# A transformer block with experts on one core: all TensorE instructions held to the order of the program

## The chip, the cores and the metric

The kernel runs on one core of a Trainium2 chip. The core has five engines, each with its own queue of instructions: TensorE (PE, matmuls and transposes; PEld is its load of weights), VectorE (DVE), ScalarE (ACT), GpSimd (POOL) and SyncE (SP), which issues most of the transfers. The engines wait for each other by semaphores. The metric is the device time of one execution in microseconds (us), the median over several executions.

## The reference

The reference takes 512 tokens of 1024 features in fp32 through two hybrid layers and a third block:

```python
for l in range(2):
    x = x + 0.5 * swiglu_ffn(rms_norm(x, ffn1_norm_w[l]), ffn1_w_gate[l], ffn1_w_up[l], ffn1_w_down[l])
    x = x + hybrid_mixer(rms_norm(x, mix_norm_w[l]), l, w_in[l], w_out[l], ...)
    x = x + 0.5 * swiglu_ffn(rms_norm(x, ffn2_norm_w[l]), ffn2_w_gate[l], ffn2_w_up[l], ffn2_w_down[l])
```

`hybrid_mixer` projects the input, runs three branches beside each other (an mLSTM in chunks of 64, a state space model in chunks of 128, and differential attention with normalised q and k) and projects them back. The third block holds a token mixer, which is a gated delta rule in two directions (in each chunk of 64 a triangular system is solved, then states are carried from chunk to chunk) beside a pooling over a grid with windows of 2, 4, 8 and 16, a second delta rule over a context of 256 tokens that gives the states to begin with, and 16 experts, each of which takes the tokens that chose it most (twice 512 tokens over 16 experts, so 64 each).

## The kernel before

Every fp32 factor is held as two rounded parts, hi and lo, and each product takes three matmuls: hi by hi (L69), lo by hi (L70), hi by lo (L71), all in `mm3`. A projection (`fm_proj`) is 8 steps over the features by three, 24 matmuls of 128x512. `tok_proj` (L238 to L240) is the same with the operands exchanged. ACT casts each chunk of weights to hi (L39), DVE takes the difference lo (L40).

`scaled_x` (L138) prepares a normalised layer: ACT casts the scaled x (L146), DVE makes lo (L147), ACT squares x (L151), POOL adds the squares up (L155). `token_stats` sums them over the partitions on PE (L106, first one sum, then the other), DVE forms the inverse root (`rsqrt`, L81 to L88), `token_rows` brings it back to rows on PE (L120), and ACT copies it to `rb` (L128). The projections don't need `rb`, only their evictions do.

In `mixer` the first four projections are q and k. After each, DVE scales it (L321), ACT squares it (L323) and PE sums the squares by head (L325). `rows()` transposes small statistics (L355). The branches are generators which `Side.pump` advances by a step, placed by hand into the stream of projections: attention (L772 QK, L782 and before it the softmax, L758 the transposes two units later, L744 the product with v), the state space model, the mLSTM. At the end `turn()` transposes the results and the output projections follow.

In ffn2 of the second layer the side work is `context`: gates (L1195 transposes, then a chain of DVE instructions, L902, L903 and L914 on PE) and the solves. A solve runs on DVE row by row, writes its blocks to memory (L1069), reads them back in another layout (L1080), and multiplies them on PE in 64x64 matmuls (L1089, L1107, L1117); `delta_scan` carries the states (L1134). `token_mixer` does the same for the 512 tokens, with the pooling (L1341, L1358, L1378, L1379) beside it. `mixer_out` transposes the scan's output (L1430), which POOL leaves at L1426. `moe` gathers tokens (L1605), multiplies them with chunks of 1 MB (L1643), for which there are 17 places, and combines the results (L1661).

What sets the order: the program is traced by Python, and a scheduler then orders each engine's instructions. It takes the instruction traced first when several are ready by its own estimate of times, and lets one that is traced later pass one that it believes to be waiting. So the order of PE before is the scheduler's. Each queue runs in its order: a waiting matmul holds what is behind it.

Of the kernel before, what the change touches and what calls it, by code (L numbers as in the profile page):

```python
# [28 lines left out]
class G:  # L29
    pass  # L30

# [68 lines left out]
def token_stats(g, sqs, nt, pool):  # L100
# [3 lines left out]
    for j, sq in enumerate(sqs):  # L104
        for i in range(nt):
            nc.tensor.matmul(ps[:, 2 * i:2 * i + 2], sq[:, i * 128:(i + 1) * 128], g.ones[:, 0:2],  # L106
                             start=(i + j == 0), stop=False, skip_group_check=True)
# [7 lines left out]
def token_rows(g, rt):  # L115
# [3 lines left out]
    for i in range(nt):  # L119
        g.nc.tensor.matmul(pb[:, i * 128:(i + 1) * 128], bc(rt[:, i:i + 1], [128, 128]), g.ident, start=True, stop=True)  # L120
# [104 lines left out]
def tok_proj(g, xh, xl, w, cols, pump=lambda: None):  # L225
# [5 lines left out]
    for wh, wl in w:  # L231
        n = wh.shape[1]
        for i in range(NT):
            ts = slice(i * 128, (i + 1) * 128)
            o = ps[i][:, :cols]
            for k in range(n):
                kk = k0 + k
                nc.tensor.matmul(o, xh[:, kk, ts], wh[:, k, :], start=(kk == 0), stop=False)  # L238
                nc.tensor.matmul(o, xh[:, kk, ts], wl[:, k, :], start=False, stop=False)  # L239
                nc.tensor.matmul(o, xl[:, kk, ts], wh[:, k, :], start=False, stop=(kk == NK - 1))  # L240
# [49 lines left out]
def mixer(g, L, w_in, w_out):  # L290
# [25 lines left out]
    for e in range(2):  # L316
        w = chunk(256)
        for m in range(2):
# [5 lines left out]
            for i in range(NT):  # L324
                nc.tensor.matmul(pst[:, 16 * i + 4 * t:16 * i + 4 * t + 4], sq[:, i * 128:(i + 1) * 128], g.blk,  # L325
# [20 lines left out]
    def rows(v, name):  # L346
# [7 lines left out]
        for i in range(NT):  # L354
            nc.tensor.transpose(pt[0:2 * n, i * 128:(i + 1) * 128], f32(parts[:, i]).rearrange("p a b -> p (a b)"),  # L355
# [4 lines left out]
    def scale_qk():  # L360
        drT = rows(drn, "dr")
        yield
        for t in (2, 3, 0, 1):
            p = sm(g)
            nc.tensor.matmul(p, g.sel16[:, t, :], drT, start=True, stop=True)
# [16 lines left out]
    def gates():  # L382
# [10 lines left out]
        for i, m in enumerate((g.triu, g.ones)):  # L393
            nc.tensor.matmul(pc[:, 48 * i:48 * i + 48], m, dl.rearrange("p c h -> p (c h)"), start=True, stop=True)
# [92 lines left out]
    def turn(k):  # L487
        p = sm(g)
        for i in range(NT):
            nc.tensor.transpose(p[:, i * 128:(i + 1) * 128], ys[k // 2][:, i, (k % 2) * 128:(k % 2 + 1) * 128], g.ident)  # L490
# [27 lines left out]
def ssd(g, V, fm, G, ys):  # L518
# [7 lines left out]
    def product(todo):  # L526
# [4 lines left out]
        for hh in range(8):  # L531
            nc.tensor.matmul(py[:, hh * 64:(hh + 1) * 64], es[hh // 4][:, hh % 4, :], xc[:, hh, :],
                             start=True, stop=True)
        nc.vector.tensor_add(y, y, py)
        if c0:
            po = sm(g)
            for q in range(2):
                nc.tensor.matmul(po[:, q * 256:(q + 1) * 256], fm[6 + q][:, c0 * 128:(c0 + 1) * 128],
# [4 lines left out]
        if c0 < NT - 1:  # L543
            pst = sm(g)
            for q in range(2):
                nc.tensor.matmul(pst[:, q * 256:(q + 1) * 256], bt[:, q, :], xcd[:, 4 * q:4 * q + 4, :],
# [9 lines left out]
    for c in range(NT):  # L556
# [3 lines left out]
        for t in range(4):  # L560
            nc.tensor.transpose(px[:, t * 128:(t + 1) * 128], fm[t][:, ts], g.ident)
# [4 lines left out]
        if c < NT - 1:  # L566
            pb = sm(g)
            for q in range(2):
                nc.tensor.transpose(pb[:, q * 128:(q + 1) * 128], fm[4 + q][:, ts], g.ident)
# [7 lines left out]
        for q in range(2):  # L577
            nc.tensor.matmul(pcb[:, q * 128:(q + 1) * 128], fm[4 + q][:, ts], fm[6 + q][:, ts], start=True, stop=True)
# [3 lines left out]
        for q in range(2):  # L582
            pa = sm(g)
            e = g.scr()[:, :S].rearrange("p (h d) -> p h d", h=4)
            nc.tensor.matmul(pa.rearrange("p (h d) -> p h d", h=4), g.eye_r, bc(g.neg_r[:, None, :], [128, 4, 128]),
                             start=True, stop=False, skip_group_check=True)
            for h in range(4):
                hh = 4 * q + h
                nc.tensor.matmul(pa[:, h * 128:(h + 1) * 128], bc(g.stk8[:, hh:hh + 1], [128, 128]), acT[:, ts],
# [35 lines left out]
def mlstm(g, gt, G, qk, vx, ycat):  # L625
# [5 lines left out]
    for i in range(NT):  # L631
        nc.tensor.transpose(pt[0:4, i * 128:(i + 1) * 128], a[:, i, :], g.ident)
# [6 lines left out]
    for i in range(NT):  # L639
        nc.tensor.transpose(pg[:, 4 * i:4 * i + 4], Gr[:, i * 128:(i + 1) * 128], g.ident[0:4, 0:4])  # L640
# [7 lines left out]
    def product(h, P):  # L648
        pn = sm(g)
        for i in range(NT):  # L650
            for j in range(i + 1):
                nc.tensor.matmul(pn[:, 66 * i:66 * i + 66], P[j][:, (i - j) * 128:(i - j + 1) * 128], vx[:, j, h, :],
# [11 lines left out]
    for e in range(2):  # L664

        pGs = []
        for h in (2 * e, 2 * e + 1):
            pG = sm(g)
            nc.tensor.matmul(pG, bc(g.stk4[:, h:h + 1], [128, 128]), Gs, start=True, stop=True)
# [4 lines left out]
        for j in range(NT):  # L674
# [3 lines left out]
            for r in range(2):  # L678
                pr = slice(64 * r, 64 * r + 64)
                pq = sm(g)  # L680
                nc.tensor.matmul(pq[:, :W], qk[1, e][pr, js], qk[0, e][pr, j * 128:], start=True, stop=True)
# [37 lines left out]
def attention(g, V, ks, qkd, dv, ycat):  # L719
# [17 lines left out]
    for n in range(len(units) + 3):  # L737
        if n >= 3:
# [4 lines left out]
            for j in range(i + 1):  # L743
                nc.tensor.matmul(po[:, h * 64:(h + 1) * 64], aT[:, j * 128:(j + 1) * 128], dv[:, j, h, :],  # L744
# [7 lines left out]
        if 2 <= n < len(units) + 2:  # L752
# [4 lines left out]
            for j in range(i + 1):  # L757
                nc.tensor.transpose(pT[:, j * 128:(j + 1) * 128], pr[:, j * 128:(j + 1) * 128], g.ident)  # L758
# [3 lines left out]
        if n < len(units):  # L762
# [7 lines left out]
            for e in range(2):  # L770
                p = sm(g)
                nc.tensor.matmul(p[:, :W], qt[0:96, h // 2, 2 * (h % 2) + e], ks[2 * h + e][0:96, 0:W],  # L772
# [25 lines left out]
def modulation(g, I):  # L798
# [14 lines left out]
    for b in range(3):  # L813
# [11 lines left out]
        for i, acc in enumerate(accs):  # L825
# [6 lines left out]
            for j in range(4):  # L832
                nc.tensor.matmul(p[32 * j:32 * j + 32, 0:16], fold, r[:, j:64:4], start=True, stop=True)
# [39 lines left out]
def delta_gates(g, ab, nt, pool, pre):  # L873
# [26 lines left out]
    for i, src in enumerate((a, rest)):  # L900
        for d, tri in ((0, g.triu), (1, g.tril)):
            nc.tensor.matmul(pv[:, 0, i, :, 4 * d:4 * d + 4], tri, src[:, :, 4 * d:4 * d + 4], start=True, stop=True)  # L902
        nc.tensor.matmul(pv[:, 1, i], g.ones, src, start=True, stop=True)  # L903
# [9 lines left out]
    for i in range(nt):  # L913
        nc.tensor.transpose(pt[0:32, i * 128:(i + 1) * 128], f32(parts[:, i]).rearrange("p a b -> p (a b)"), g.ident)  # L914
# [31 lines left out]
def prep_keys(g, kraw, nt, P, kt, kf):  # L946
# [4 lines left out]
    for h in range(4):  # L951
        sq = P["scr"]()[:, :nt * 128]
        nc.scalar.activation(sq, kraw[h], AF.Square)
        for c in range(nt):
            nc.tensor.matmul(pq[:, 4 * c + h:4 * c + h + 1], sq[:, c * 128:(c + 1) * 128], g.ones[:, 0:1],
# [1093 lines left out]
```

## Time and profile before

| | us |
|---|---|
| median of 3 executions | 3054.05 (3049.53 to 3057.12) |
| profiled execution | 3055.56 |
| its span | 3053.5 |
| mean granted TensorE clock | 0.969 |

The span is the time from the first to the last instruction of the profiled execution; 2.06 us lie outside it. The granted clock is a share of the full 2.4 GHz. Stretches by start: ffn1 of the first layer to 396 us, its mixer to 686, ffn2 from 690, the second layer's ffn1 from 1059, its mixer from 1427, ffn2 with the context from 1724, the token mixer from 2166, its output and the routing from 2460, the experts from 2572 us.

### The profile page before, as it was taken

The page shows a single profiled execution, that of the slowest core. Times are in us where ns is not written, and L with a number is a line of the kernel's source. Part 1 is how long each engine was busy: PE and PEld are TensorE (multiplying, and loading weights), DVE is VectorE, ACT ScalarE, POOL GpSimd, SP SyncE. Part 2 cuts the span into 40 slices and gives each one's busy share as a digit, 9 for nine tenths or more (in the row PEclk, how much of TensorE's full clock was granted, in tenths as well). Part 3 has the DMA queues.
Part 4 walks back from the last instruction along what each step waited for, and adds up shares of the span by engine and source line. Part 5 has one row for each costly group of instructions (what it writes and reads, how often), then busy time and mean ns, then how long its engine had stood idle before and what let it go on. Part 6 is the DMA issues. An engine that isn't in the chain of part 4 may idle for free. (4 is left out here: it accounts for less than half of the span.)

```text
span 3053.5 us, 37758 instructions
## 1 busy us (share of the span) xinstructions
PE 2905.0 (95%) x15232; PEld 2225.9 (73%) x15232; DVE 1636.6 (54%) x2847; ACT 905.5 (30%) x1515; POOL 321.4 (11%) x260
## 2 busy tenths in 40 slices
PE   7999998999999999999999999999998877999998
PEld 6888887877888888888776788888787765444444
DVE  4445457665444598545676666454765643122213
ACT  3222334543222332223354433222342321010002
POOL 0001012110201102011210201201100110000000
PEclk9999999999999999999998999999999978999998
DMA  4432343122332358224421233222323435999996
GB/s 146 126 100 92 104 147 116 52 85 84 97 97 94 113 197 297 99 93 135 128 76 56 93 114 104 84 85 90 114 66 94 116 142 201 394 419 418 418 418 277
DMA packets 293107, 472.03 MB, mean 155 GB/s; under 512 B 45215, under 2 KB 237471, under 8 KB 269508
## 3 DMA queue, kind: packets, MB, share of 16 engines
q1 hardware_dynamic: 290216, 466.28, 43.4%
q10 hardware_dynamic: 2716, 3.34, 0.3%
q8 instruction: 120, 1.97, 0.3%
q14 instruction: 55, 0.45, 0.0%
HBM read 449.90 MB, written 19.67 MB: 154 GB/s over the span
## 5 line engine op out<-in xcount | busy, mean ns | idle before, releaser
L69 PE MATMUL mm<-xh,whi 128*128 128x512 f32 x1952 | 777.0, 400 | 12.0 <-ACT xh L146 8.4
L70 PE MATMUL mm<-xl,whi 128*128 128x512 f32 x1952 | 774.9, 397 | 0.6 <-DVE xl L147 0.6
L71 PE MATMUL mm<-xh,wlo 128*128 128x512 f32 x1952 | 772.5, 396 | 1.7 <-DVE wlo L40 1.7
L39 ACT CAST whi<-wraw 128x1024 fp32r<-128x1024 f32 (+3 forms) x390 | 390.9, 1003 | 1113.8 <-PE mm L70 831.4
L40 DVE TENSOR_TENSOR wlo<-wraw,whi 128x1024 fp32r<-128x1024 f32 (+3 forms) x390 | 501.6, 1286 | 97.5 <-ACT whi L39 90.5
L69 PEld LDWEIGHTS mm<-xh,whi 128*128 128x128 f32 x1952 | 372.5, 191 | 92.2 <-ACT xh L146 9.3
L70 PEld LDWEIGHTS mm<-xl,whi 128*128 128x128 f32 x1952 | 372.9, 191 | 82.0 <-issue 3.8
L71 PEld LDWEIGHTS mm<-xh,wlo 128*128 128x128 f32 x1952 | 372.4, 191 | 80.6 <-DVE wlo L40 3.3
L69 PE MATMUL mm<-hh,whi 128*128 128x512 f32 x704 | 279.4, 397 | 0.0
L70 PE MATMUL mm<-hl,whi 128*128 128x512 f32 x704 | 278.7, 396 | 0.0
L71 PE MATMUL mm<-hh,wlo 128*128 128x512 f32 x704 | 278.4, 395 | 0.0
L192 POOL TENSOR_TENSOR x<-x,dt 128x512 f32<-128x512 f32 x72 | 125.7, 1746 | 859.7 <-DVE dt L191 766.0
L172 DVE TENSOR_TENSOR gs<-mm,rb 128x512 f32<-128x512 f32 x88 | 60.8, 691 | 202.5 <-PE mm L71 198.2
L191 DVE SCALAR_TENSOR_TENSOR dt<-mm,rb 128x512 f32<-128x512 f32 x104 | 71.8, 690 | 179.8 <-PE mm L71 179.8
L177 DVE TENSOR_TENSOR gs<-gs,mm 128x512 f32<-128x512 f32 x88 | 60.4, 686 | 196.9 <-PE mm L71 196.8
L71 PEld LDWEIGHTS mm<-hh,wlo 128*128 128x128 f32 x704 | 132.2, 188 | 31.9
L70 PEld LDWEIGHTS mm<-hl,whi 128*128 128x128 f32 x704 | 132.2, 188 | 31.7 <-DVE hl L40 0.3
L69 PEld LDWEIGHTS mm<-hh,whi 128*128 128x128 f32 x704 | 132.2, 188 | 31.6
L1643 PE MATMUL mm<-e_raw,e_x 128*64 128x512 f32 x504 | 118.9, 598 | 0.0
L238 PE MATMUL mm<-whi,xh 128*128 128x512 f32 (+2 forms) x288 | 104.0, 361 | 0.0
L239 PE MATMUL mm<-wlo,xh 128*128 128x512 f32 (+2 forms) x288 | 100.2, 348 | 0.0
L240 PE MATMUL mm<-whi,xl 128*128 128x512 f32 (+2 forms) x288 | 100.2, 348 | 0.0
(646 smaller groups left out, 3561.6 us busy)
## 6 DMA issues: line engine op xcount, KB each, us to landing
wraw<-ffn_gate SPq DMA_DIRECT2D x44, 1024.0 KB, 5.4
wraw<-ffn_up SPq DMA_DIRECT2D x44, 1024.0 KB, 5.3
wraw<-w_in SPq DMA_DIRECT2D x38, 1024.0 KB, 5.3
e_raw<-e_gate SPq DMA_DIRECT2D x36, 1024.0 KB, 12.6
e_raw<-e_up SPq DMA_DIRECT2D x27, 1024.0 KB, 15.0
e_raw<-e_down SPq DMA_DIRECT2D x25, 1024.0 KB, 14.3
wraw<-ffn_down SPq DMA_DIRECT2D x24, 1024.0 KB, 5.1
mw<-w_mod SPq DMA_DIRECT2D x24, 1024.0 KB, 5.0
```

The source lines that it names most:

```text
L39: g.nc.scalar.copy(hi, src)
L40: g.nc.vector.tensor_sub(lo, src, f32(hi))
L69: g.nc.tensor.matmul(out, lh, rh, start=first and i == 0, stop=False, skip_group_check=not (first and last))
L70: g.nc.tensor.matmul(out, lh, rl, start=False, stop=False, skip_group_check=not (first and last))
L71: g.nc.tensor.matmul(out, ll, rh, start=False, stop=last and i == n - 1, skip_group_check=not (first and last))
L172: nc.vector.tensor_mul(gs, pg, rb)
L191: nc.vector.scalar_tensor_tensor(t, pd, 0.25, rb, op0=OP.mult, op1=OP.mult)
L192: (nc.vector if c0 + nch == sum(groups) else nc.gpsimd).tensor_add(g.x[2 * c + m], g.x[2 * c + m], t)
L238: nc.tensor.matmul(o, xh[:, kk, ts], wh[:, k, :], start=(kk == 0), stop=False)
L239: nc.tensor.matmul(o, xh[:, kk, ts], wl[:, k, :], start=False, stop=False)
L240: nc.tensor.matmul(o, xl[:, kk, ts], wh[:, k, :], start=False, stop=(kk == NK - 1))
L1643: nc.tensor.matmul(ps[h][pj[j], :], lhs(k, j), raw[j][:, h * 512:(h + 1) * 512], start=(k == 0), stop=(k == NK - 1), skip_group_check=True)
```

## The change

A small wrapper stands for TensorE. Each matmul or transpose that is issued through it is handed to `keep_in_program_order`, which ties it to the instruction traced before it on the same engine, for the order of issue alone, with no semaphore. The scheduler can't let one pass another any more, so PE's order is the order in which Python traced it. All calls of the kernel are replaced in the same way; three are shown. In the kernel after, all PE instructions carry the wrapper's line, L41, and other lines are 11 higher (12 from the end of `body` on).

```diff
+class InOrder:
+
+
+    def __init__(self, tc, engine):
+        self.tc, self.engine = tc, engine
+
+    def __getattr__(self, name):
+        f = getattr(self.engine, name)
+        return lambda *a, **k: self.tc.keep_in_program_order(f(*a, **k))
...
-        g.nc.tensor.matmul(out, lh, rh, start=first and i == 0, stop=False, skip_group_check=not (first and last))
-        g.nc.tensor.matmul(out, lh, rl, start=False, stop=False, skip_group_check=not (first and last))
-        g.nc.tensor.matmul(out, ll, rh, start=False, stop=last and i == n - 1, skip_group_check=not (first and last))
+        g.pe.matmul(out, lh, rh, start=first and i == 0, stop=False, skip_group_check=not (first and last))
+        g.pe.matmul(out, lh, rl, start=False, stop=False, skip_group_check=not (first and last))
+        g.pe.matmul(out, ll, rh, start=False, stop=last and i == n - 1, skip_group_check=not (first and last))
...
     g.nc, g.tc = tc.nc, tc
+    g.pe = InOrder(tc, tc.nc.tensor)
     nc = tc.nc
```

The same 12602 instructions stand on PE before and after. The orders of the other engines move by a few places, since the scheduler's estimates change.

The first place is the head of the first mixer, PE, before (sm_2577 is the sum of squares, sm_2603 the broadcast rows, mm_2649 and mm_2681 the first two projections):

```order
L106 MATMUL sm_2577<-cst_96,x_2546 128x2 x4
L69 MATMUL mm_2649<-xh_2544,whi_2641 128x512
L70 MATMUL mm_2649<-xl_2545,whi_2641 128x512
L71 MATMUL mm_2649<-xh_2544,wlo_2642 128x512
...
L106 MATMUL sm_2577<-cst_96,x_2546 128x2 x4
L70 MATMUL mm_2649<-xl_2545,whi_2641 128x512
...
L120 MATMUL sm_2603<-cst_96,rt_2588 128x128 x4
L71 MATMUL mm_2649<-xh_2544,wlo_2642 128x512
L69 MATMUL mm_2681<-xh_2544,whi_2645 128x512
```

The same place on PE after the change:

```order
L41 MATMUL sm_2577<-cst_96,x_2546 128x2 x8
L41 MATMUL sm_2603<-cst_96,rt_2588 128x128 x4
L41 MATMUL mm_2649<-xh_2544,whi_2641 128x512
L41 MATMUL mm_2649<-xl_2545,whi_2641 128x512
L41 MATMUL mm_2649<-xh_2544,wlo_2642 128x512
```

Both sums and the rows moved ahead of the first projection; 23 matmuls that stood among them stand behind.

The second place is the token mixer's gates, PE, before (t_scr holds the gates' projections, t_a and t_rest the parts of the logarithms, t_parts the sums):

```order
L1195 MATMUL sm<-cst,t_scr 128x16 x4
...
L902 MATMUL sm<-t_a,cst 128x4x4
L902 MATMUL sm<-t_a,cst_12568 128x4x4
L903 MATMUL sm<-t_a,cst 128x32
...
L902 MATMUL sm<-t_rest,cst 128x4x4
L902 MATMUL sm<-t_rest,cst_12568 128x4x4
L903 MATMUL sm<-t_rest,cst 128x32
...
L914 MATMUL sm<-cst,t_parts 32x128 x4
```

The same place on PE after the change:

```order
L41 MATMUL sm<-cst,t_scr 128x16 x4
L41 MATMUL sm<-t_a,cst 128x4x4
L41 MATMUL sm<-t_a,cst_12568 128x4x4
L41 MATMUL sm<-t_a,cst 128x32
L41 MATMUL sm<-t_rest,cst 128x4x4
L41 MATMUL sm<-t_rest,cst_12568 128x4x4
L41 MATMUL sm<-t_rest,cst 128x32
L41 MATMUL sm<-cst,t_parts 32x128 x4
```

The 34 projections between L1195 and the first L902, and those behind it, moved behind L914.

The third place is the token mixer's second solve, PE, before (sm_18138 is the first product of the solved blocks, mm_18127 a product of the pooling, mm_18185 to mm_18188 projections of the `tok_proj` kind):

```order
L1358 MATMUL mm_18127<-t_yp_17238,t_pw_18080 128x512
L238 MATMUL mm_18185<-whi_18167,xh_16149 128x512
L239 MATMUL mm_18185<-wlo_18168,xh_16149 128x512
L240 MATMUL mm_18185<-whi_18167,xl_16150 128x512
...
L1089 MATMUL sm_18138<-x_16522,x_16520 64x64
...
L1089 MATMUL sm_18138<-x_16522,x_16520 64x64 x15
```

The same place on PE after the change:

```order
L41 MATMUL mm_18127<-t_yp_17238,t_pw_18080 128x512
L41 MATMUL sm_18138<-x_16522,x_16520 64x64 x16
L41 MATMUL mm_18185<-whi_18167,xh_16149 128x512
L41 MATMUL mm_18185<-wlo_18168,xh_16149 128x512
L41 MATMUL mm_18185<-whi_18167,xl_16150 128x512
```

The sixteen products moved ahead of the fifty projections that stood before the first of them.

## Rows read from the trace of the kernel before

**Rows 1.** The page, part 1: busy us (share of the span) xinstructions of each engine.
```profile
PE 2905.0 (95%) x15232; PEld 2225.9 (73%) x15232; DVE 1636.6 (54%) x2847; ACT 905.5 (30%) x1515; POOL 321.4 (11%) x260
```

**Rows 2.** Table by stretch: us, PE, PEld, DVE, ACT, POOL busy, PEclk, DMA, GB/s.
```profile
463.00:468.70 5.70, 5.53 (x16) 4.22 (x17) 3.35 (x6) 2.90 (x5) 3.31 (x4) 0.50 0.71 239
473.00:554.00 81.00, 75.73 (x397) 61.52 (x396) 61.11 (x165) 42.59 (x105) 14.01 (x12) 1.00 0.29 90
2284.00:2345.00 61.00, 47.17 (x659) 43.43 (x658) 38.76 (x108) 18.16 (x30) 5.20 (x8) 0.92 0.38 93
2460.00:2572.00 112.00, 72.36 (x373) 61.88 (x371) 47.35 (x109) 19.30 (x34) 13.38 (x11) 0.74 0.42 160
2572.00:2800.00 228.00, 227.51 (x1172) 105.08 (x1173) 49.99 (x93) 22.06 (x41) 0.00 (x0) 1.00 0.97 398
```

**Rows 3.** Timeline, first mixer's head: start us, us, engine line op [idle before <-releaser].
```profile
397.35 0.62 ACT L151 ACTIVATE x<-x 128x512 f32<-128x512 f32 x1
399.24 0.39 PE L69 MATMUL mm<-xh,whi 128*128 128x512 f32 x1
399.47 0.95 PE L106 MATMUL sm<-cst,x 128*128 128x2 f32 x8
402.64 0.16 DVE L88 SCALAR_TENSOR_TENSOR rt<-rs_t,rs_i 128x4 f32<-128x4 f32 x1
402.86 1.16 PE L120 MATMUL sm<-cst,rt 128*128 128x128 f32 x8
```

**Rows 4.** Timeline, head of the first layer's ffn2.
```profile
690.32 1.33 PE L69 MATMUL mm<-xh,whi 128*128 128x512 f32 x3 [4.25 <-ACT xh L146]
694.54 1.72 POOL L155 TENSOR_TENSOR x<-x 128x512 f32<-128x512 f32 x1 [4.49 <-ACT x L151]
702.59 1.11 PE L120 MATMUL sm<-cst,rt 128*128 128x128 f32 x8
```

**Rows 5.** Timeline, second projection of the first mixer.
```profile
405.64 0.68 DVE L321 TENSOR_TENSOR fmt<-mm,rb 128x512 f32<-128x512 f32 x1
406.36 0.63 ACT L323 ACTIVATE scr<-fmt 128x512 f32<-128x512 f32 x1 [1.52 <-DVE fmt L321]
407.04 1.05 PE L325 MATMUL sm<-cst,scr 128*128 128x4 f32 x8
```

**Rows 6.** Timeline of PE, first mixer, around the row transposes.
```profile
463.17 1.02 PE L355 MATMUL sm<-cst,ac_p 128*16 128x128 f32 x4 [3.10 <-DVE ac_p L40]
...
464.42 0.63 PE L69 MATMUL mm<-xh,whi 128*128 128x512 f32 x1
464.84 0.63 PE L70 MATMUL mm<-xl,whi 128*128 128x512 f32 x1
```

**Rows 7.** Timeline of PE, gates of the context.
```profile
1792.64 0.30 PE L1195 MATMUL sm<-cst,c_scr 16*128 16x16 f32 x2
...
1800.82 0.58 PE L902 MATMUL sm<-c_a,cst 128*128 128x8 f32 x4 [0.20 <-DVE c_a L894]
```

**Rows 8.** Timeline of SP's queue and of PE, second solve of the context.
```profile
2002.52 2.62 SPq L1080 DMA_DIRECT2D c<-ds  x4
2006.44 0.30 PE L1089 MATMUL sm<-c,c 64*64 64x64 f32 x2 [0.88 <-DMA c<-ds]
```

**Rows 9.** Timeline of PE, gates of the token mixer.
```profile
2209.18 0.42 PE L1195 MATMUL sm<-cst,t_scr 16*128 16x16 f32 x4
...
2217.44 0.59 PE L902 MATMUL sm<-t_a,cst 128*128 128x16 f32 x4
```

**Rows 10.** Timeline of PE, second solve of the token mixer.
```profile
2385.49 2.08 PE L1358 MATMUL mm<-t_yp,t_pw 128*128 128x512 f32 x2 [6.44 <-DVE t_yp L1383]
...
2400.33 0.33 PE L1089 MATMUL sm<-x 64*64 64x64 f32 x2
```

**Rows 11.** Timeline of PE, two later waits of the token mixer.
```profile
2327.57 0.45 PE L1089 MATMUL sm<-x 64*64 64x64 f32 x2 [7.77 <-DMA x<-ds]
...
2470.94 1.12 PE L1430 MATMUL sm<-cst,t_raw 128*128 128x128 f32 x4 [7.33 <-POOL t_raw L1426]
```

More of the change, by code (lines that the diff above doesn't have):

```diff
@@ L119, in token_rows @@
     for i in range(nt):
-        g.nc.tensor.matmul(pb[:, i * 128:(i + 1) * 128], bc(rt[:, i:i + 1], [128, 128]), g.ident, start=True, stop=True)
+        g.pe.matmul(pb[:, i * 128:(i + 1) * 128], bc(rt[:, i:i + 1], [128, 128]), g.ident, start=True, stop=True)
     return pb[:, :nt * 128]
@@ L364, in scale_qk @@
             p = sm(g)
-            nc.tensor.matmul(p, g.sel16[:, t, :], drT, start=True, stop=True)
+            g.pe.matmul(p, g.sel16[:, t, :], drT, start=True, stop=True)
             nc.vector.scalar_tensor_tensor(qf[t], qf[t], V["qk_w"][:, t // 2:t // 2 + 1], p,
@@ L668, in mlstm @@
             pG = sm(g)
-            nc.tensor.matmul(pG, bc(g.stk4[:, h:h + 1], [128, 128]), Gs, start=True, stop=True)
+            g.pe.matmul(pG, bc(g.stk4[:, h:h + 1], [128, 128]), Gs, start=True, stop=True)
             t = g.scr()[:, :S]
@@ L680, in mlstm @@
                 pq = sm(g)
-                nc.tensor.matmul(pq[:, :W], qk[1, e][pr, js], qk[0, e][pr, j * 128:], start=True, stop=True)
+                g.pe.matmul(pq[:, :W], qk[1, e][pr, js], qk[0, e][pr, j * 128:], start=True, stop=True)
                 pqs.append(pq)
@@ L901, in delta_gates @@
         for d, tri in ((0, g.triu), (1, g.tril)):
-            nc.tensor.matmul(pv[:, 0, i, :, 4 * d:4 * d + 4], tri, src[:, :, 4 * d:4 * d + 4], start=True, stop=True)
-        nc.tensor.matmul(pv[:, 1, i], g.ones, src, start=True, stop=True)
+            g.pe.matmul(pv[:, 0, i, :, 4 * d:4 * d + 4], tri, src[:, :, 4 * d:4 * d + 4], start=True, stop=True)
+        g.pe.matmul(pv[:, 1, i], g.ones, src, start=True, stop=True)
     sums = pool.tile([128, 2, 2, nt, 8], F32, name=pre + "sums", bufs=1)
@@ L954, in prep_keys @@
         for c in range(nt):
-            nc.tensor.matmul(pq[:, 4 * c + h:4 * c + h + 1], sq[:, c * 128:(c + 1) * 128], g.ones[:, 0:1],
+            g.pe.matmul(pq[:, 4 * c + h:4 * c + h + 1], sq[:, c * 128:(c + 1) * 128], g.ones[:, 0:1],
                              start=True, stop=True)
@@ L1017, in inner @@
             hs = slice(h * 128, (h + 1) * 128)
-            nc.tensor.matmul(p[:, hs], kf[c][:, hs], rhs(h, hs), start=True, stop=True)
+            g.pe.matmul(p[:, hs], kf[c][:, hs], rhs(h, hs), start=True, stop=True)
         if kept is None:
@@ L1088, in blocks @@
             for hf in halves:
-                nc.tensor.matmul(p[hf, m, :], lhs(hf, m), rhs[hf, m, :], start=True, stop=True, skip_group_check=True)
+                g.pe.matmul(p[hf, m, :], lhs(hf, m), rhs[hf, m, :], start=True, stop=True, skip_group_check=True)
         return p
@@ L1133, in four @@
             hs = slice(h * 128, (h + 1) * 128)
-            nc.tensor.matmul(p[:, hs], lhs(h, hs), rhs(h, hs), start=True, stop=True)
+            g.pe.matmul(p[:, hs], lhs(h, hs), rhs(h, hs), start=True, stop=True)
         return p
@@ L1340, in token_mixer @@
         for i in range(NT):
-            nc.tensor.matmul(pq[:, 4 * i + h:4 * i + h + 1], sq[:, i * 128:(i + 1) * 128], g.ones[:, 0:1],
+            g.pe.matmul(pq[:, 4 * i + h:4 * i + h + 1], sq[:, i * 128:(i + 1) * 128], g.ones[:, 0:1],
                              start=True, stop=True)
@@ L1357, in pooled @@
         p = g.ps_m.tile([128, 512], F32, name="mm")
-        nc.tensor.matmul(p, pws[q], yp[:, q, :], start=True, stop=True)
+        g.pe.matmul(p, pws[q], yp[:, q, :], start=True, stop=True)
         nc.scalar.activation(yp[:, q, :], p, AF.Copy, scale=v["pool_scale"][:, q:q + 1])
@@ L1567, in moe @@
             for j in range(NK):
[L1568 removed]
+                g.pe.matmul(ps[:, 0:16], bc(shift[:, j:j + 1], [128, 128]), wr[:, j, :], start=(j == 0),
                                  stop=(j == NK - 1))
@@ L1939, in spread @@
         p = sm(g)
-        nc.tensor.matmul(p[0:4, :k], rbt, oh[:, c:c + k], start=True, stop=True)
+        g.pe.matmul(p[0:4, :k], rbt, oh[:, c:c + k], start=True, stop=True)
         nc.vector.tensor_copy(row[:, c:c + k], p[0:4, :k])
@@ L1949, in spread @@
         p = sm(g)
-        nc.tensor.matmul(p, g.exch, m, start=True, stop=True)
+        g.pe.matmul(p, g.exch, m, start=True, stop=True)
         m2 = P.tile([128, S], F32, name="bflip", bufs=2)
```

95 lines of the change are left out of this document (47 added, 48 removed).

## The prediction

> **What bounds the kernel now.** I read the busy times first: the matrix engine PE works for 95% of the span, and no other engine for more than 54% [rows 1]. The reader is to see that any time in which PE must wait, where it has not waited before, goes onto the span unless a later wait gives it back. Then the table by stretch [rows 2] tells where PE waits already: hardly at all in the feed-forward layers, 5.3 us (81.00 - 75.73) of the first attention stretch, 13.8 us of the stretch of the token mixer's first solve, 40 us between the token mixer and the experts, which are limited by transfers: over 2572 to 2800 us the DMA engines are busy for 0.97 of the time. So a delay ahead of 2572 us moves the first gather of the experts, and with it every chunk of weights that waits for a place, and so the end. The timeline at each place where the order of PE differs tells the rest: what PE did while a result was on its way.
>
> **What the change does.** No instruction is added or taken away. The order of PE differs in 64 stretches, and in nearly all of them the same thing happens: a matmul that waits for a result of another engine stood, before, behind as many independent matmuls as the result took; now it stands right behind what it follows in the program, and those independent matmuls stand behind it. The cover goes; PE stands still for the length of the chain, and the covering matmuls are then done at their usual pitch of 0.23 us (399.24 to 399.47 us, [rows 3]). So the price of a moved wait is the lesser of two numbers: the chain, and the number of covering matmuls by 0.23 us.
>
> **1. Heads of the six normalised layers.** Sums of squares (L106), a chain of DVE instructions for the root, and the broadcast of it (L120) stood among the first projections. In the first mixer 23 projections lie around them; now all of them come after L120. The last square ends at 397.97 us (397.35 + 0.62, [rows 3]); 0.95 for the second L106, 2.4 for the chain (400.42, where L106 ended, to 402.80) and 1.16 for L120 put the first projection at about 402.4, and 23 by 0.23 us end at 407.7, where before they were done at 403.8 to 404.1: 3.6 us. The head of the second layer's ffn1 and that of its mixer are alike (3.6, 3.5), and the first head of all, with 15 projections, 4. In ffn2 the squares come later: POOL's last addition ends at 696.26 [rows 4], so L120 ends at about 701.5 where the first projection was at 690.32; of 13 us of PE's work 36 projections (8.3 us) must now follow: 7 us. ffn2 of the second layer has the same head and the context's own rows behind it, with 24 more projections of cover: 10.8. Sum 32.5; from 20 (chains shortened because DVE has nothing else to do) to 45 (the covers in full).
>
> **2. Square sums of q and k (L325), and the row transposes (L355).** After the fourth of a group of projections, DVE scales it (0.68 us from 405.64) and ACT squares it (0.63), and L325 starts at 407.04 [rows 5]. Now PE waits for that at once: 407.04 - 405.64 = 1.4, and 0.2 for the end of the matmul: 1.6 us, eight times, 12.8 us. L355 waits for 3.10 us already [rows 6] and loses one or eight covering matmuls more, 1.9 us in each layer: 3.8. Sum 16.6, from 8 to 20.
>
> **3. Attention.** The first QK product moves from 484.45 us to right behind the matmul at 472.7, and from there on a unit of attention and 12 projections alternate as written. That is 2.7 us of projections and about 1 us of attention, against a chain of 6 to 7 us from QK to the transposed probabilities, which is used two units later: 2 by 3.7 = 7.4 us. It just fits, and DVE is busy for 61.11 of 81 us [rows 2]. I take 4 us in each layer, 8 in all; from -6 (the first unit starts 11.7 us earlier) to +30 (every unit waits for DVE).
>
> **4. mLSTM and the output projections.** 32 projections that ran between the last steps of the recurrence now stand behind them: at most 32 by 0.23 = 7.4 us in each layer, at least 0, since they fill waits that the trace shows later on. I take 4, twice: 8.
>
> **5. The context's work beside ffn2 of layer two.** From the end of L1195 (1792.94) to L902 (1800.82) 33 projections hide the chain for the gates [rows 7]: 7.5, with the six before the next wait 8.9; I take 8.5. In its second solve, 40 projections hide the way of the solved blocks to memory and back ([rows 8]: the last read is issued at 2002.52, the result used at 2006.44): 40 by 0.23 = 9.1. Two smaller ones 2.0, the remaining short steps 2.4. Sum 22, from 12 to 27.
>
> **6. Token mixer.** Its gates repeat this with 34 covering projections [rows 9]: 7.7 and, for the two waits behind, 1.3, so 9. The second solve loses the most: after L1358 at 2385.49, fifty matmuls fill the time until the solved blocks are back at 2400.33 [rows 10]; they now stand behind L1089: 50 by 0.23 = 11.4. The first solve loses 82 short matmuls of 0.12 us and 16 of 0.23 (13.5 us), but 7.77 us that PE waited later [rows 11] have less before them, and the later gaps of the stretch are filled: 6. Then come 1.3 for one more chain and, at the tail, 35 projections (8 us) that move behind the scan into a wait of 7.33 us for POOL [rows 11], where they cost nothing, but had covered the scan's steps: 1.5. Sum 29; from 5 (the 40 and 13.8 us of idle time of [rows 2] take up most of it) to 45.
>
> **7. Experts.** Gather and combination change places with matmuls of the pair before, which costs PE up to 1 us a pair; the transfers hide it. The start of the pipeline loses 3 us, from 0 to 6.
>
> **8. The clock.** After L355 has waited for 3.10 us, the following matmuls come at a pitch of 0.42 us (464.42, 464.84) instead of 0.23 [rows 6], and the granted clock from 463 to 468.7 us is 0.50 [rows 2], the lower of its two levels (1.2 of 2.4 GHz). That is some 13 matmuls by 0.2 = 2.5 us for a wait. Of the new waits I count four that are as long and whose neighbourhood was at the full clock, and take 2 us each: 8, from 0 to 25. The Trainium skill, "TensorE: Matmul & The Clock Gate", section "HAM oscillation — how this bites in real kernels", says that waits between bursts of matmuls throw TensorE back to the lower clock again and again, and speaks against this change. Of the short waits the trace says otherwise: attention has waits of about 1 to 2 us and a granted clock of 1.00 [rows 2].
>
> **Less.** While PE waits it gives DVE nothing to evict. In the chain of the context's gates 1.9 us of 7.9 are DVE's work for others. Six such chains by 2 us: -12.
>
> The sum: 32.5 + 16.6 + 8 + 8 + 22 + 29 + 3 + 8 - 12 = 115 us. On the profiled run of 3055.56 (2.06 us outside its span) that is 3171; against the median shown, 1.5 lower, 3169. I say 3170.
>
> **Rivals.** *Given back.* The new waits make PE late, but DVE, ACT and the transfers are then ahead, so later waits shrink: the 40 us ahead of the experts, the 5 us of each attention, the idle time of the solves. For it: PE is idle for some 150 us in all. Against it: in the feed-forward layers there is none to give back, and terms 1, 2 and 5 lie before such. Keeping half of terms 1, 2 and 5 (36) and the clock (8), and nothing of the rest: 3056 + 44 = 3100.
>
> *Not slower.* The waiting matmuls are the heads of the long chains, and none is queued behind projections any more. If attention starts 11.7 us earlier in each layer and ends earlier by as much, and the solves and the scan, beside which PE stands still for 53 us in two stretches [rows 2], go ahead undisturbed, then 2 by 11.7 + 30 = 53 us are won against terms 1, 2 and 5, of which the lower bounds (20 + 8 + 12 = 40) remain: 3056 - 13 = 3043. It decides from the point where the chain from the scan's last step to POOL's L1426 starts earlier, counted from the start of the token mixer, by more than 30 us. Against it: before, a waiting matmul was seldom later than its data by more than one projection.
>
> *Lockstep.* Attention waits for DVE in each of its 19 units, 1 us more than counted, in two layers: 38. The recurrence takes its upper bound, 15 instead of 8: 7. The clock falls at the short waits as well, and takes its upper bound, 25 instead of 8: 17. 3170 + 62 = 3232. For it: DVE at 61 of 81 us in attention. The clock falling at each short wait is part of this case.
>
> *No effect* is excluded: the order of PE as built differs in the places named.
>
> **How the numbers follow.** Forecast (3130 to 3230) 0.68; given back (3065 to 3130) 0.17; lockstep (above 3230) 0.09; not slower 0.06. A measurement of this kernel can't tell less than 0.3% (9 us) from no change. Faster holds most of the last case, 0.04; within 0.3% its rest and the edge of "given back", 0.03; slower 0.93. The range from 3095 to 3235 leaves out the last case, half of "given back" at most and what lies above: 2 in 10.
>
> **What would show it.** Right: at each layer's head a wait of 2 to 6 us ahead of L120 and one of about 1.5 us ahead of each sum of L325; waits of about 8 us ahead of L902, twice, of 9 us and 11 us ahead of L1089; the same matmul durations; experts that take as long as before, from a later start. Wrong: the feed-forward layers' ends no later than 60 us in sum by the end of the context's work (2166 us before), or the first gather of the experts no later than before.

## The result and the profile after

The kernel after takes 3243.15 us (median of 3, 3242.18 to 3243.46), the kernel before 3054.05: a ratio of 1.0615, with a 95% interval from 1.0599 to 1.0632. It is slower by 189 us, where I had said 115, and lies outside the range. The profiled execution has a span of 3240.0 us and a mean granted clock of 0.940 (before 3053.5 and 0.969).

Part 1 of the page of the kernel after, the line that answers to [rows 1]:

```profile
PE 2942.0 (91%) x15232; PEld 2274.6 (70%) x15232; DVE 1649.0 (51%) x2847; ACT 907.4 (28%) x1515; POOL 319.2 (10%) x260
```

The same 15232 records on PE are busy for 37 us more, and PE stands still for 298 us, where it was 148.5. The longer span is 149.5 us of waits and 37 us of slower matmuls. Ahead of the experts the matmuls' records are longer by 50 us and the waits by 134. Among the experts, where the DMA engines are busy for 0.97 of the time [rows 2], the records are shorter by 13 us and the waits longer by 16.

Where it went is found by lining up the two traces: at every place up to which both kernels have issued the same instructions on PE, the end of the last of them is compared. What is added between two such places belongs to the stretch between them:

| stretch | foretold (term) | measured | of it waits | of it slower matmuls |
|---|---|---|---|---|
| heads of six layers | 32.5 (1) | 48.5 | 32.7 | 15.8 |
| sums of q and k, row transposes | 16.6 (2) | 24.8 | 15.8 | 9.0 |
| attention | 8 (3) | 29.6 | 16.5 | 13.1 |
| recurrence, output projections | 8 (4) | 6.6 | 12.0 | -5.4 |
| context | 22 (5) | 31.2 | 23.8 | 7.4 |
| token mixer | 29 (6) | 38.0 | 29.4 | 8.6 |
| routing, experts | 3 (7) | 7.8 | 19.0 | -11.3 |
| clock | 8 (8) | within the rows above | | in each row |
| less | -12 | within the rows above | | |
| sum | 115 | 186.5 | 149 | 37 |

The bodies of the three feed-forward layers without the context add 0.0 us each. The table of stretches of PE alone shows both halves of the loss (columns: us, PE busy (records), granted clock, share of the DMA engines, GB/s). The kernel before, in the first mixer's head, its q and k, its attention, and the token mixer's gates:

```profile
396.10:404.00 7.90, 7.90 (x44) 1.00 1.05 364
404.00:426.40 22.40, 22.40 (x119) 1.00 0.31 96
469.20:553.70 84.50, 79.23 (x412) 1.00 0.30 92
2208.00:2237.60 29.60, 29.60 (x167) 0.94 0.17 55
```

The kernel after, in the same places, with the body of a feed-forward layer as the fourth row:

```profile
400.50:415.50 15.00, 11.08 (x44) 0.66 0.55 195
415.50:448.70 33.20, 27.22 (x119) 0.86 0.20 64
493.00:593.00 100.00, 86.58 (x413) 0.90 0.24 74
1126.00:1485.90 359.90, 359.65 (x1601) 1.00 0.48 161
2351.80:2402.50 50.70, 36.86 (x167) 0.73 0.10 31
```

In the head, the same 44 records were without a gap in 7.90 us; now they are busy for 11.08 of 15 us. 3.9 us are waits, as worked out (3.6). The other 3.2 us are matmuls at a granted clock that has fallen from 1.00 to 0.66 on average. In the stretch of q and k it is 6.0 us of waits and 4.8 of slower matmuls. The timeline of PE in the kernel after shows how, first at the head, against [rows 3]:

```profile
402.43 1.87 PE L41 MATMUL sm<-cst,x 128*128 128x2 f32 x8 [1.48 <-ACT x L162]
406.73 2.07 PE L41 MATMUL sm<-cst,rt 128*128 128x128 f32 x8 [2.44 <-DVE rt L99]
...
409.03 0.63 PE L41 MATMUL mm<-xl,whi 128*128 128x512 f32 x1
409.45 0.63 PE L41 MATMUL mm<-xh,wlo 128*128 128x512 f32 x1
...
412.20 0.39 PE L41 MATMUL mm<-xh,whi 128*128 128x512 f32 x1
412.43 0.39 PE L41 MATMUL mm<-xl,whi 128*128 128x512 f32 x1
```

Behind two waits of 1.48 and 2.44 us the projections come at a pitch of 0.42 us until 411.6, and only then at 0.23. Then at the first sum of q, against [rows 5]:

```profile
417.21 1.05 PE L41 MATMUL sm<-cst,scr 128*128 128x4 f32 x8 [1.45 <-ACT scr L334]
...
419.07 0.63 PE L41 MATMUL mm<-xh,whi 128*128 128x512 f32 x1
419.49 0.63 PE L41 MATMUL mm<-xl,whi 128*128 128x512 f32 x1
```

The wait is 1.45 us (I had 1.4, and 0.2 for the matmul's end), and within a microsecond behind the sum the clock falls for some seven matmuls. The same holds behind the second and the fourth sum, but not behind the third, though PE waits 1.55 us ahead of it. The waits of PE by what they are for (us in total, times, longest) in the kernel after:

```profile
PE sm L41 <- DVE rt L99: 28.2, 8, 5.5
PE sm L41 <- ACT scr L334: 12.0, 8, 1.6
PE sm L41 <- DMA c<-ds: 10.2, 2, 10.0
PE sm L41 <- DVE t_a L905: 5.7, 1, 5.7
PE sm L41 <- ACT t_scr L964: 5.6, 1, 5.6
PE sm L41 <- DVE c_a L905: 5.6, 1, 5.6
```

These are the waits that were foretold: the roots ahead of the broadcast rows, the squares of q and k eight times, the context's solve (10.0; 9.1 foretold), and both gates (5.6 and 5.7, where about 8 was foretold). The fifth line I had not counted: the squares of the keys, behind the token mixer's gates. The second solve of the token mixer, against [rows 10], and the last transposes, against [rows 11]:

```profile
2554.65 2.07 PE L41 MATMUL mm<-t_yp,t_pw 128*128 128x512 f32 x2 [8.01 <-DVE t_yp L1394]
2565.09 2.50 PE L41 MATMUL sm<-x 64*64 64x64 f32 x32 [8.37 <-DMA x<-ds]
...
2653.74 3.04 PE L41 MATMUL sm<-cst,t_raw 128*128 128x128 f32 x13 [2.60 <-POOL t_raw L1437]
```

The solve's wait is 8.37 us (11.4 foretold), and the wait of 7.33 us for POOL is down to steps of 2.6 and less, as foretold. In the scan ahead of it PE waits 7.7 us longer than before.

### The profile page after: what moved, and what is told of

Read it like the earlier page. It is cut to its first block, busy times and chain, and to the rows that moved or that the text cites. A ratio compares the mean times of both kernels' runs of the same rounds, so it can differ in the third digit from the quotient of the medians.

```text
span 3240.0 us, 37754 instructions
## 1 busy us (share of the span) xinstructions
PE 2942.0 (91%) x15232; PEld 2274.6 (70%) x15232; DVE 1649.0 (51%) x2847; ACT 907.4 (28%) x1515; POOL 319.2 (10%) x260
## 5 line engine op out<-in xcount | busy, mean ns | idle before, releaser
L41 PE MATMUL mm<-xh,whi 128*128 128x512 f32 x1952 | 790.6, 405 | 2.7 <-ACT xh L864 2.2
L41 PE MATMUL mm<-xl,whi 128*128 128x512 f32 x1952 | 780.7, 400 | 2.5 <-DVE xl L51 1.8
L41 PE MATMUL mm<-xh,wlo 128*128 128x512 f32 x1952 | 778.7, 399 | 0.0
L41 PEld LDWEIGHTS mm<-xh,whi 128*128 128x128 f32 x1952 | 379.8, 195 | 88.5 <-issue 5.6
L41 PEld LDWEIGHTS mm<-xl,whi 128*128 128x128 f32 x1952 | 379.1, 194 | 83.8 <-DVE xl L51 2.7
L41 PEld LDWEIGHTS mm<-xh,wlo 128*128 128x128 f32 x1952 | 378.3, 194 | 81.7
L41 PE MATMUL mm<-hh,whi 128*128 128x512 f32 x704 | 280.0, 398 | 0.0
L41 PE MATMUL mm<-hl,whi 128*128 128x512 f32 x704 | 278.8, 396 | 0.0
L41 PE MATMUL mm<-hh,wlo 128*128 128x512 f32 x704 | 278.7, 396 | 0.0
L41 PEld LDWEIGHTS mm<-hh,wlo 128*128 128x128 f32 x704 | 132.5, 188 | 32.3
L41 PEld LDWEIGHTS mm<-hh,whi 128*128 128x128 f32 x704 | 132.5, 188 | 31.9
L41 PEld LDWEIGHTS mm<-hl,whi 128*128 128x128 f32 x704 | 132.6, 188 | 31.8 <-DVE hl L51 0.3
L41 PE MATMUL mm<-e_raw,e_x 128*64 128x512 f32 x504 | 110.9, 593 | 0.0
L41 PE MATMUL mm<-whi,xh 128*128 128x512 f32 (+2 forms) x288 | 104.0, 361 | 0.0
L41 PE MATMUL mm<-whi,xl 128*128 128x512 f32 (+2 forms) x288 | 100.9, 350 | 0.0
L41 PE MATMUL mm<-wlo,xh 128*128 128x512 f32 (+2 forms) x288 | 100.5, 349 | 0.0
```

What stands on the lines that cost most here:

```text
L41: return lambda *a, **k: self.tc.keep_in_program_order(f(*a, **k))
```

## The experiments

The theory: each moved wait costs its cover, and the clock that falls behind it; stretches don't touch each other. The rivals stand with each run. "The in-order kernel" is the kernel after the change. The delay at a place is how much later PE gets there than in the kernel before, read by lining up two traces as above.

**Matmuls that nobody reads, in the waits** of the in-order kernel:

```diff
+def fill(g, out, n, start=True):
+    for _ in range(n):
+        g.pe.matmul(out, g.ident, g.ident, start=start, stop=start, skip_group_check=True)
...
+        if j:
+            fill(g, ps[:, 128:256], 5, False)
...
+    fill(g, pb[:, 0:128], 10)
...
+            fill(g, pst[:, 128:256], 6)
```

> In-order kernel, in which small matmuls of the identity, whose result nobody reads, are put into the waits of PE at the layers' heads (5 between the two sums of squares, 10 ahead of the broadcast rows) and ahead of the sums of q and k (6 each). Nothing is moved, so each result comes when it came. Theory (cover lost, and TensorE's clock falls at each such wait, short ones too): PE isn't idle there, the granted clock of the q and k stretch goes from 0.86 to above 0.97 and that of the heads from 0.66 to above 0.85, and the 26 us by which PE's busy time grew in these stretches come back for the most part: 20 us faster than the in-order kernel, about 3223. Rival (the matmuls behind a wait are slow because their data or weights come late, and the clock has no part in it): same or up to 8 us slower, 3243 to 3251.

Measured: 3217.91 us, 1.0528 [1.0510, 1.0545] of before, 25 us faster than the in-order kernel. Table of stretches of this run, the first mixer's head and its q and k:

```profile
400.80:412.70 11.90, 11.54 (x75) 1.00 0.68 246
412.70:442.90 30.20, 29.58 (x178) 1.00 0.23 71
```

and the timeline at the same two places:

```profile
406.21 1.16 PE L41 MATMUL sm<-cst,rt 128*128 128x128 f32 x8
...
414.30 1.05 PE L41 MATMUL sm<-cst,scr 128*128 128x4 f32 x8
```

No matmul is moved and PE has more to do, and still the kernel is faster, with the granted clock at 1.00 in both stretches. The rival, in which the clock has no part, had the same time or a longer one. So the slower matmuls at the heads and sums are the clock, and in these places it costs about 25 us, as the last column of the table has it (15.8 and 9.0).

**The cover written by hand** into the program of the in-order kernel, at the heads and the sums of q and k:

```diff
-                pg = fm_proj(g, xh, xl, wg[m])
+                pg = fm_proj(g, xh, xl, wg[m], pump=stats if rb is None else None)
+                if rb is None:
+                    _, rb = finish()
...
+            p = fm_proj(g, xh, xl, w[m], pump=None if t else stats)
+            if t:
+                if t == 1:
+                    pst = sm(g)
+                sums(t - 1)
+            else:
+                rt, rb = finish()
```

> In-order kernel with the program written so that the cover stands in it: the sums of squares come in the middle of the first projection, the broadcast rows behind it, the sums of q and k one projection later. Theory: what the in-order kernel lost at six heads (less the context's own rows), 45 us, and at the sums of q and k, 21 us, comes back: 3243 - 66 = 3177 (3168 to 3188). Rival (given back: without these waits DVE and the transfers are less far ahead, and later waits grow): half of it, about 3210.

Measured: 3171.36 us, 1.0377 [1.0357, 1.0396]: 72 us come back, where 66 were foretold. Up to the end of the first layer's sums of q and k the delay is under 1 us, where it was 19.5. Nothing of what is won is lost again later. The 6 us above the forecast are found in attention (3 us in each layer), which this edit doesn't touch: there the same matmuls are mostly faster.

**Order held in the mixers alone**, and left to the scheduler elsewhere, as in the kernel before (the diff is against the in-order kernel):

```diff
-    g.pe = InOrder(tc, tc.nc.tensor)
+    g.pe = tc.nc.tensor
...
+                    g.pe = InOrder(tc, tc.nc.tensor)
                     mixer(g, L, I["w_in"][L], I["w_out"][L])
+                    g.pe = tc.nc.tensor
```

> Kernel before, in which only the matmuls of the two mixers are held to the order of the program. Theory (each stretch loses its own cover, and none touches another): the ledger of the in-order kernel gives 39 us for the first mixer and 36 for the second: 3054 + 75 = 3129 (3121 to 3137). Rival (the losses add up only because the scheduler's estimates go wrong more and more along the program): less than 60 us, below 3114.

Measured: 3128.93 us, 1.0239 [1.0224, 1.0254]: 74 us slower than the kernel before, as the sum over the two mixers has it (39 and 36). The delay made in the mixers stays to the end, in a program whose other parts are the scheduler's.

**Attention a unit deeper**, in the in-order kernel:

```diff
-    for n in range(len(units) + 3):
-        if n >= 3:
-            i, h = units[n - 3]
+    for n in range(len(units) + 4):
+        if n >= 4:
+            i, h = units[n - 4]
...
-        if 2 <= n < len(units) + 2:
-            i, h = units[n - 2]
+        if 3 <= n < len(units) + 3:
+            i, h = units[n - 3]
```

> In-order kernel, in which attention's transposes follow three units behind the QK products instead of two, and the products with v four. Theory (in the fixed order PE waits for the chain from QK to the probabilities): the waits for the probabilities, 7.7 us in the first layer (one of 6.2), go, and the clock is kept up longer: 8 to 11 us in each layer, 3243 - 19 = 3224. Rival (DVE is the bound of attention, and a place in PSUM or a later unit makes PE wait instead): within 5 us, 3238 to 3248.

Measured: 3222.67 us, 1.0546 [1.0530, 1.0562], 20 us faster than the in-order kernel. In the in-order kernel, the timeline of PE has in the first layer

```profile
508.84 0.47 PE L41 MATMUL sm<-cst,scr 128*128 128x128 f32 x1 [6.17 <-DVE scr L793]
```

and with the deeper attention the waits of PE between 493 and 590 us are

```profile
PE sm L41 <- DVE amx L785: 6.4, 4, 3.9
PE sm L41 <- ACT scr L771: 2.5, 2, 2.3
```

The waits for the probabilities are gone; those for the reduction of QK (amx) stay, and are about 6 us in both. With the two traces lined up, 16 of the 20 us come back in the two mixers, half of them by shorter waits and half by faster matmuls (granted clock 0.96 from 493 to 590 us, where it was 0.90 from 493 to 593). So about half of the 29.6 us was the depth that was too small for a fixed order.

**The gates in steps**, in the in-order kernel (a yield ahead of L902 and of L914 as well):

```diff
-    run(features(1552, 4, 4, raw, "t_raw"))
-    ab = delta_ab(...)
...
-    gates = delta_gates(g, ab, NT, P, "t_")
+    side.add(make_gates())
+    run(features(1552, 4, 4, raw, "t_raw"), 1)
+    side.drain()
```

> In-order kernel in which the gates' work of the context and of the token mixer is traced in steps with projections between them (the side work yields ahead of L902 and ahead of L914; the token mixer's gates run beside its first four projections, not behind them). Theory (the gates lost their cover, 33 and 34 projections): the context's gates give back 9 of the 12 us that they cost, the token mixer's 11 of 21, since the wait for the squares of the keys behind them, 5.6 us, stays: 3243 - 20 = 3223 (3215 to 3231). Rival (the token mixer's 21 us are the keys' and the scan's chain, and the gates only wait beside it): 10 us or less, 3233 or more.

Measured: 3220.55 us, 1.0543 [1.0528, 1.0557], 23 us faster. The sum is as foretold, but not its parts: between the context's rows and the end of ffn2 17 us come back (21 are lost where it was 38), and from there to the end nothing, 46 us in both. The other 5 us lie ahead of the edit, where the two programs are the same and PE waits as long: there the matmuls were faster in this run. The timeline of PE of this run at the token mixer's gates:

```profile
2332.45 1.46 PE L41 MATMUL sm<-t_a,cst 128*128 128x16 f32 x6 [6.79 <-DVE t_a L905]
```

With 24 projections as cover PE waits 6.79 us, where it was 5.7 without: beside the first projections DVE has their convolutions to do, and the gates' chain on DVE takes 12.4 us, where it took 5.2 alone. For the token mixer the rival holds.

**The kernel before with the deeper attention**, same edit as above, order left to the scheduler:

> Kernel before (order left to the scheduler), with attention's transposes three units behind the QK products and the products with v four. Theory (the waits for the probabilities, 5.0 us in each layer, are a chain that a unit more would hide): 3054 - 8 = 3046. Rival (the scheduler hides what can be hidden, DVE is the bound): 3051 to 3057.

Measured: 3047.46 us, 0.9981 [0.9972, 0.9990]. It is 6 us faster than the kernel before, near the theory's 3046.

**The kernel before with matmuls in the wait ahead of ffn2**:

```diff
+    if g.cold:
+        fill(g, sm(g)[:, 0:128], 16)
```

> Kernel before, with 16 matmuls of the identity, which nobody reads, put into PE's wait of 4.25 us ahead of the two ffn2 layers. Theory (the clock falls in this wait, and the first twelve projections behind it run at half of it): 2.5 us each, 3054 - 5 = 3049. Rival (these projections wait for their inputs anyway, so a faster clock ends in longer waits): 3053 to 3056.

Measured: 3060.36 us, 1.0020 [1.0011, 1.0028]: slower. Table of stretches of this run, from the filling on:

```profile
685.90:697.00 11.10, 7.70 (x51) 1.00 0.13 46
697.00:704.40 7.40, 7.40 (x26) 0.54 0.00 0
```

and of the kernel before:

```profile
690.30:696.60 6.30, 6.09 (x19) 0.73 0.00 1
696.60:702.60 6.00, 6.00 (x36) 1.00 0.00 0
```

The clock is kept up at the place itself, and POOL's sum of squares comes when it came. But the edit did more than was meant, as the timelines of PE show at that sum, first in this run and then in the kernel before:

```profile
696.35 1.05 PE L112 MATMUL sm<-cst,x 128*128 128x2 f32 x8 [1.62 <-POOL x L163]
```

```profile
696.64 0.95 PE L106 MATMUL sm<-cst,x 128*128 128x2 f32 x8
```

The scheduler now puts this sum behind 12 projections, where 19 stood ahead of it. So PE waits for POOL, as it did not before, and behind that wait the clock falls: a lost cover once more. The run doesn't show what matmuls in this wait are worth when the order stays.

**The kernel before with the gates in steps**, same edit:

> Kernel before, with the gates traced in steps as in the in-order run with steps; the token mixer's come beside its first projections, some 20 us earlier. Theory (the first solve, where PE is idle for 13.8 us of 61, starts when gates and keys are there, and the gates are the later): 3054 - 8 = 3046. Rival (keys or DVE decide): 3051 to 3057.

Measured: 3054.35 us, 1.0002 [0.9993, 1.0011]: no change, as the rival had it. The gates' rows (L914) come 9.5 us earlier in the token mixer, but the first gather of the experts comes at the same time within 0.1 us.

**All covers by hand**: the three edits in one in-order kernel, and steps in the context's solve:

```diff
-    yield
+    for _ in range(4 if P["pre"] == "c_" else 1):
+        yield
```

> In-order kernel with all covers written by hand so far: heads and sums of q and k, attention a unit deeper, gates in steps, and four steps in place of one behind the read of the context's solve (two steps are taken per projection), which puts two projections into its wait of 10 us. Theory (each place has its own price): the three gains measured apart, 72 + 21 + 23, and 11 for the solve: 3243 - 127 = 3116 (3106 to 3128). Rival (the scheduler's order gains from something that no fixed order of the program has, or the gains overlap): 3140 or more.

Measured: 3137.88 us, 1.0278 [1.0264, 1.0292]: 105 us come back, 22 less than the sum. Up to the last layer's head the two edits of the mixers give 8 us less together than apart; with the steps in the solve, 15 us are lost in the context where it was 21, not 11 fewer. Another 5 us were in the forecast that were not the gates' own (the faster matmuls ahead of that run's edit). So gains measured apart add up only roughly; the time lies between theory and rival, nearer to the rival. The 45 us from the end of ffn2 on are untouched.

**Rows moved in the kernel before**, with deeper attention, and only these transposes held in order:

```diff
+        yield
+        yield
         G.update(spl=spl, acT=rows(acs, "ac"), nacs=nacs, Bc=Bc, ex=ex)
...
+            if name == "ac":
+                g.tc.keep_in_program_order(turned)
```

> Kernel before with attention a unit deeper, and the row transposes of the mixers' gates (L355, which PE waits 3.1 us for) moved behind two more half projections and these transposes alone held to the order of the program. Theory (the scheduler believed their input ready 3 us too early, and the clock fell behind the wait): 3.1 + 2.3 us in each layer less than the kernel with deeper attention alone: 3047 - 10 = 3037. Rival (as with the matmuls put ahead of ffn2, PE arrives sooner at the next wait): 3045 to 3050.

Measured: 3051.79 us, 0.9993 [0.9984, 1.0002]. Table of stretches of PE in this run, and then a line of PE's waits between 440 and 560 us:

```profile
455.00:475.00 20.00, 20.00 (x94) 1.00 0.65 195
```

```profile
PE sm L776 <- DVE amx L778: 8.2, 2, 6.3
```

In the kernel before, the first of these reads

```profile
455.00:475.00 20.00, 16.89 (x68) 0.83 0.62 188
```

The 3.1 us and the half clock are gone from the place itself, as meant; but attention's first reduction on DVE comes 2.7 us later than before (487.40 for 484.71), and PE waits 6.3 us for one of these reductions. What was won is given back, and more, since with the deeper attention alone it was 3047: this is the rival, a little above its range. Why DVE comes later was not followed.

**The token mixer and all that follows left to the scheduler**, the rest in order:

```diff
+            g.pe = tc.nc.tensor
             with tc.tile_pool(name="dp", bufs=1) as g.dp:
                 y = token_mixer(g, I)
```

> In-order kernel, in which the matmuls from the token mixer on (token mixer, its output, experts) are left to the scheduler again. Theory (each stretch loses its own cover): the 46 us that the in-order kernel lost between the end of ffn2 and the end come back: 3243 - 46 = 3197 (3191 to 3203). Rival (the steps of the gates gave nothing back here, so the token mixer's loss is carried in from the context's late end, and stays): 3225 or more.

Measured: 3191.83 us, 1.0454 [1.0437, 1.0470]: 51 us come back, where 46 were foretold. Some 45 of them come back from the token mixer on, so the loss is made there and not carried in. The others lie ahead of it, where the two programs are the same. The stretches of PE up to the token mixer, first in this run and then in the in-order kernel, are

```profile
0.00:2180.00 2180.00, 2020.01 (x9654) 0.95 0.33 105
```

```profile
0.00:2186.00 2186.00, 2025.84 (x9655) 0.95 0.33 105
```

The waits are the same to a few tenths, and the records of the same matmuls are 5.8 us shorter. So what the slower matmuls cost differs by some 5 us between two kernels ahead of the place where they differ; why stays open, and a gain of that size means little here.

**Attention two units deeper** in the kernel before:

> Kernel before with attention's transposes four units behind the QK products and the products with v five. Theory (some of the waits for the probabilities, 3.5 us in sum, are left with three units): 3 us less than with three, 3044. Rival (the last units, which have no projections beside them any more, come later by a unit, and eat it): the same as with three or more, 3047 to 3052.

Measured: 3049.00 us, 0.9987 [0.9979, 0.9996]; with one unit 0.9981 [0.9972, 0.9990]. No difference between the two can be told, which is the rival.

## Why the prediction was wrong

The sign, the places and most of the mechanism were right: a moved wait costs its cover. The waits came near their terms too: at the heads 32.7 us against 32.5, at the sums and transposes 15.8 against 16.6, in the context 23.8 against 22. Of my signs, the experts took as long as before within 4 us, from a later start; "the same matmul durations" failed. Ahead of the experts the loss is 184 us, where the terms without the experts' 3 had 112. Of the 72 us between them 42 are slower matmuls (50 for 8), and 30 are waits (134, where the terms less 12 had 104).

**The step that failed is the clock, term 8.** I counted four long waits and gave them 8 us, since attention before has waits of 1 to 2 us at a granted clock of 1.00 [rows 2]. From that I took it that short waits don't lower it. The kernel after shows a fall behind a wait of 1.45 us, and a mean of 0.86 over the four sums of q and k and 0.90 over attention. Slower matmuls are 50 us ahead of the experts, and the run with matmuls in the waits shows that 25 of them, at heads and sums, are the clock. For the other 25 the granted clock of the same stretches speaks (attention 0.90 for 1.00, the token mixer's gates 0.73 for 0.94), but no run separates it there.

The trace of the kernel before could have told it. I read the attention of one layer; the same wait stands in both, here in the timeline of PE:

```profile
510.15 0.44 PE L758 MATMUL sm<-cst,scr 128*128 128x128 f32 x2 [2.04 <-DVE scr L782]
510.68 0.40 PE L69 MATMUL mm<-xh,whi 128*128 128x512 f32 x1
510.91 0.40 PE L70 MATMUL mm<-xl,whi 128*128 128x512 f32 x1
...
1540.57 0.66 PE L758 MATMUL sm<-cst,scr 128*128 128x128 f32 x2 [2.06 <-DVE scr L782]
...
1541.45 0.63 PE L69 MATMUL mm<-xh,whi 128*128 128x512 f32 x1
1541.88 0.63 PE L70 MATMUL mm<-xl,whi 128*128 128x512 f32 x1
```

Behind 2.04 us in the first layer the pitch stays at 0.23 us; behind 2.06 us in the second it is 0.43, and the granted clock from 1540.6 to 1544.0 us is 0.50. So the length of a wait alone doesn't tell whether the clock falls. What else decides it, in these two and at the third of the four sums, stays open. The sentence of the Trainium skill that I set aside ("TensorE: Matmul & The Clock Gate", section "HAM oscillation — how this bites in real kernels": TensorE goes back to its lower clock between bursts) speaks of longer waits, for transfers; the trace shows the same here, at 0.86 on average, behind shorter ones.

**Attention, term 3,** was 8 and is 29.6, of which 13.1 are slower matmuls in the two layers. The sum of units against the chain "just fits", I wrote, and left out that DVE takes the evictions and convolutions in its own order ahead of the softmax. In the kernel after, PE is done with the first QK product at 496.9 us, and DVE's first reduction of it starts at 506.19:

```profile
496.56 0.34 PE L41 MATMUL sm<-fmt,x 96*128 96x128 f32 x2
...
506.19 0.28 DVE L785 CUSTOM_DVE_ANT_0 scr<-sm,bias 128x128 f32<-128x128 f32 x1
```

That is the one wait of 6.2 us in each layer. The lockstep case had both kinds of loss (38 for the units, 17 for the clock), with a time of 3232 and a chance of 0.09; it was the nearest of the cases, though not every unit waits.

**"Less", -12,** was there only in part. At both gates the two waits that had lost their cover are 6.6 us (5.62 and 0.96) against covers of 8.9, and 6.8 (5.74 and 1.07) against 9.0: about 2 us less each, as taken off. At the heads the waits are not shorter (32.7 against 32.5). At the token mixer's gates it doesn't help: 21 us are lost there in all, 13.8 of them waits, of which 5.6 are for the squares of the keys, a second chain behind the first that I had not followed in the new order.

**Given back** fails for the loss: what the cover written by hand and the free token mixer won stays to the end. In the kernel before it fits two edits: gates that came 9.5 us earlier gave nothing at the end, and a wait taken away ahead of attention came back as another. In the second of them PE met a result of DVE that came later than before. Between the heads, where PE waits for nothing else, one more wait is lost for good.

## What to carry to other kernels

An order fixed by the program is only as good as the cover that stands in the program: for each matmul that waits for another engine, ask what was issued in that time, and write it there before the order is fixed. A wait of PE costs its length and, behind it, often some matmuls at the half clock: slower matmuls were about a quarter of the loss here (50 of 186 us). Read the granted clock by stretch, not over the span, and in every place where a wait recurs, not in one. Small matmuls that nobody reads brought back 25 us of that part here, where the order was fixed. Where it was the scheduler's, putting them in moved other matmuls as well, and the kernel became 6 us slower.

## What the runs showed of the hardware that was not expected

Behind a wait of only 1.45 us the pitch of 128x512 matmuls rose from 0.23 to 0.42 us for seven matmuls, with a granted clock of 0.86 over the stretch with four such waits; with PE kept busy in the same waits it was 1.00. The same wait of 2 us left the clock at 1.00 in one layer and at 0.50 in the next. The same matmuls in the same order, up to the token mixer, took PE 5.8 us longer in one kernel than in another whose program differs only behind them.
